# A third row pair of gate and up in seven products, and the sum T of each block's outer pairs in a tile of its own

## The chip, the cores and the metric

One NeuronCore of a Trainium2 chip runs the whole program. The metric is the time of one execution on the device in microseconds (us), the median of several runs.

## The reference

A trunk of two residual layers on 256 tokens of width 2048, in float32. Each layer has a token mixer (a gated linear recurrence in layer 0, gated linear attention in layer 1) with a cross-attention beside it, an output projection, and a SwiGLU feed-forward part. The change touches the feed-forward part alone:

```python
D_MODEL = 2048
SEQ = 256
DEPTH = 2
D_FF = ((8 * D_MODEL // 3 + 255) // 256) * 256        # 5632

    for layer in range(DEPTH):
        ...
        hn = _rmsnorm(h, norm_ffn[layer])
        gate, up = jnp.split(hn @ w_gate_up[layer], 2, axis=-1)
        h = h + (jax.nn.silu(gate) * up) @ w_down[layer]
    return _rmsnorm(h, norm_final)
```

`w_gate_up` is 2048 x 11264 in each layer, `w_down` 5632 x 2048.

## The kernel before

**Matmuls.** Every float32 operand is split into a high part and the rest (`split`: ACT copies the high part in the rounded matmul type, DVE subtracts it). A product of two such operands takes three matmuls: high by high, high by rest, rest by high. Tokens are the stationary side, in 128 x 128 blocks; weights are the moving side, 512 columns wide.

**Gate and up.** `ffn` goes through 11 blocks of 512 columns of gate and the 512 columns of up that belong to them (`up_block`, `project_halves`). A block is a sum over 8 row pairs, each of 256 rows of the weights: two rows of 128 by two columns (gate c0, up c1), against two rows of tokens. Done plainly such a 2 x 2 by 2 x 2 product takes eight products of blocks. `KINDS` has a letter for each row pair of a block: S takes seven products (a Strassen scheme in Winograd's form, with sums and differences of the blocks), O and H take eight in two ways that end in the same seven sums. `KINDS[min(b, 4)]` is used, so blocks 4 to 10 share the last string. `PAIRS` says which combinations of the tokens are made ready for each row pair (`Forms`, 8 factors for S, 6 for O).

**A row pair in seven products.** `load_pair` fills a tile `raw` of four 512-wide columns: raw 0 and 3 are gate's two rows, raw 1 and 2 up's. The scheme needs T, the sum of up's two rows: SP loads the first row into raw 1, and POOL then issues a DMA that adds the second row to it in memory (`accum_op`, line 424), which has to wait until the first has landed. SP loads raw 0, 3 and 2 as well. `seven` then makes four splits, named a to d in the tiles: a and b of weights as loaded, then two subtractions in `raw` (the first reads T), then c (from raw 0 and T, with the sign turned) and d. So DVE has six operations for a pair in seven products and two for a plain O pair. Tiles are numbered by `n_w`, which counts every weight tile: `parts139c` is split c of weight tile 139, the pair whose loads go to `raw139`.

**Buffers.** There are three `raw` tiles in turn, six `parts` tiles (1024 wide, both parts), two `part` tiles (512 wide, split a alone). Eight PSUM banks hold the seven sums of a block (`f_p`) and the accumulators of the down projection (`fd`).

**Down projection.** After each block of gate and up stand two pieces of the down projection (`down`), each 2 x 4 weight rows onto a 512-wide part of h. ACT first copies h into the banks (`fd<-h`) and at the end back (`h<-fd`). The block's seven sums are added up on DVE (`sums`, `s` and `e`), gated (`gate`), and turned for later pieces. One of the subtractions of the down weights' splits goes to POOL (line 292, `free_port`), ordered behind the first of the sums.

**Order of work.** Each engine works through its queue in order. `mark` and `due` put the pieces at fixed keys, and `Engine.kept` has PE, DVE and ACT keep the written order in the blocks. DMAs issued from SP and from POOL stand in those engines' queues where a scheduler puts them, and a DMA whose wait is not over holds what is queued behind it.

The tile tag `scx` has one buffer. In the mixers it holds scores; in the feed-forward part it is not used.

Of the kernel before, what the change touches and what calls it, by code (L numbers as in the profile page):

```python
# [9 lines left out]
F32 = mybir.dt.float32  # L10
# [7 lines left out]
P = 128  # L18
T = 256
# [21 lines left out]
def trunk_kernel(ctx: ExitStack, tc: tile.TileContext, x, mem, norm_mix, norm_ffn, norm_mem,  # L41
# [234 lines left out]
    def split(src, name, by=2, turned=False):  # L276

        n, m = src.shape[1:]
# [81 lines left out]
    PAIRS = "SSOSSOSB"  # L360
# [51 lines left out]

    def load_pair(raw, w, p, c0, c1, n, kind, fed):

        if n_w[0] == 1:
            for k, j, c in ((0, 0, c0), (0, 1, c1), (1, 3, c0), (1, 2, c1)):
                nc.sync.dma_start(out=raw[:, j, 0:n], in_=w[(2 * p + k) * P:(2 * p + k + 1) * P, c:c + n])
                if k == 0 and c == c1:
                    load_mem(0, 256, 512)
            return  # L420
        if kind == "S" and fed:
            rows = [w[(2 * p + k) * P:(2 * p + k + 1) * P, c1:c1 + n] for k in range(2)]
            nc.sync.dma_start(out=raw[:, 1, 0:n], in_=rows[0])
            nc.gpsimd.dma_start(out=raw[:, 1, 0:n], in_=rows[1], accum_op=ALU.add)  # L424
        nc.sync.dma_start(out=raw[:, 0:4:3, 0:n], in_=w[2 * p * P:(2 * p + 2) * P, c0:c0 + n].rearrange("(k p) c -> p k c", p=P))
        if kind == "S" and fed:
            nc.sync.dma_start(out=raw[:, 2, 0:n], in_=rows[1])
        else:
            nc.sync.dma_start(out=raw[:, 1:3, 0:n], in_=w[2 * p * P:(2 * p + 2) * P, c1:c1 + n].rearrange("(k p) c -> p k c", p=P))

    def seven(i, raw, fed, between=None):
# [10 lines left out]
        tt(out=raw[:, 0, :], in0=raw[:, 1, :], in1=raw[:, 0, :], op=ALU.subtract)  # L442
        tt(out=raw[:, 2:4, :], in0=raw[:, 2:4, :], in1=raw[:, 0:1, :].broadcast_to([P, 2, n]), op=ALU.subtract)
        t6, t7 = split(raw[:, 0:2, :], f"{i}c", turned=True)
# [158 lines left out]
    def project_halves(forms, kinds, w, c0, c1, name, key, keep):  # L603
# [15 lines left out]
        for p, kind in enumerate(kinds):  # L619
            Engine.kept = keep <= p  # L620
            i, raw = new_raw()
            fed = True
# [551 lines left out]
    KINDS = ("SHOSHOSO", "HHOSSOSO", "SHOSSOSO", "SSOSSOHS", "SSOSSOSS")  # L1174
# [10 lines left out]
    def ffn(l, forms, r, after, tail=None):  # L1185
        sq = {}

        def up_block(b):
            ps = project_halves(forms, KINDS[min(b, 4)], w_gate_up[l], 512 * b, DFF + 512 * b, f"f{l}_{b}_",
                                100 * b, 0 if b else 3)  # L1190
# [55 lines left out]
        for b in range(DFF // 512):  # L1246
            up_block(b)
            todo += [(i, n) for i, part in enumerate(PARTS) if part[-1] == b - 1 for n in range(NQ)]
            for j in range(2):
                if todo:  # L1250
                    down(*todo.pop(0), 100 * b + 10 + 2 * j, 100 * b + WHEN[min(b, 3)]["back"][j])
# [150 lines left out]
```

## Time and profile before

| | |
|---|---|
| time, median of 3 runs (lowest to highest) | 2261.01 us (2260.9 to 2262.21) |
| the profiled execution: its time, its span | 2261.07 us, 2259.0 us |
| busy: PE, DVE, ACT, POOL | 99%, 87%, 63%, 9% |
| DMA | 473.60 MB, mean 210 GB/s |
| chain that ended last: PE, DVE, DMA, issue | 94%, 2%, 1%, 1% |
| blocks 4 to 9 of layer 0, start to start | 62.1 us each |
| one such block: DVE busy, ACT busy, POOL busy | 55.6, 40.1, 7.7 us |

Times in the timelines are in us from the start of the span. A row of a timeline has its start, its length, the engine, the line, the operation, what it writes and reads, the shapes, and how many were merged; in brackets, if there is one, the idle time of the engine before it and what ended that. Nearly all operations of PE, DVE and ACT have line 151, which is a helper that issues them, so rows are told apart by their tiles. The start of one row to the start of the next on the same engine is the step, a little less than the length, since the ends overlap.

### The profile page before, as it was taken

To read this page: it belongs to the slowest core of one execution; us is meant where nothing else is said; L and a number is where in the kernel's file an instruction comes from. 1 tells how busy PE (TensorE), PEld (TensorE's weight loads), DVE (VectorE), ACT (ScalarE), POOL (GpSimd) and SP (SyncE) were. 2 spreads that over 40 slices of the span, in tenths; PEclk is the share of its full clock that TensorE was granted. 3 is DMA by queue.
4 is the path that set the end of the run, shared out by engine and by line. 5 is a ranking of instruction groups with operands and counts; after the bars stand their busy time and mean duration, and the time that the engine had idled before them with its cause. 6 is when DMAs were issued, how large, how long until landed. Compare 5 with 4: busy or idle time off the path is not lost.

```text
span 2259.0 us, 30203 instructions
## 1 busy us (share of the span) xinstructions
PE 2245.2 (99%) x10710; PEld 1903.1 (84%) x10710; DVE 1974.4 (87%) x2459; ACT 1425.3 (63%) x1938; POOL 202.3 (9%) x205
## 2 busy tenths in 40 slices
PE   9999999999999999999999999999999999999998
PEld 7888888888888888888889999988888888888887
DVE  6889899898898989988986887889889898888987
ACT  7656656565666666665665665566566666666664
POOL 1000100000111111111100000000011111111110
PEclk9999999999999999999999999999999999999999
DMA  8656655665676777777765455566677777777774
GB/s 295 215 169 212 203 182 171 196 196 182 210 241 213 244 234 216 228 233 227 232 216 171 137 165 182 166 205 200 201 230 226 227 232 222 230 228 220 240 235 155
DMA packets 255691, 473.60 MB, mean 210 GB/s; under 512 B 17807, under 2 KB 47283, under 8 KB 255283
## 3 DMA queue, kind: packets, MB, share of 16 engines
q1 hardware_dynamic: 233507, 429.65, 56.8%
q0 software_dynamic: 20736, 37.76, 10.5%
q10 hardware_dynamic: 1296, 4.26, 0.5%
q8 instruction: 84, 1.38, 0.2%
q14 instruction: 68, 0.56, 0.1%
HBM read 468.45 MB, written 3.15 MB: 209 GB/s over the span
## 4 chain that ended last, share of the span: by engine, by line
PE 94%; DVE 2%; issue 1%; DMA 1%; ACT 0%; SPq 0%; POOLq 0%; DVEq 0%; POOL 0%; ACTq 0%
PE f_p L151 37%; PE fd L151 17%; PE wo L151 4%; PE m1p L151 2%; PE hv2p L151 2%; PE hv1p L151 2%; PE hv0p L151 2%; PE hf0p L151 2%; PE wo0p L151 2%; PE wo1p L151 2%; PE hf2p L151 2%; PE hf1p L151 2%; PE m0p L151 2%; PE gk0p L151 1%; PE gk1p L151 1%; PE gg11p L151 1%
## 5 line engine op out<-in xcount | busy, mean ns | idle before, releaser
L151 DVE TENSOR_TENSOR raw<-raw 128x512 f32<-128x512 f32 (+3 forms) x330 | 303.7, 921 | 49.8 <-DMA raw<-in_w_gate_up_dram 30.9
L151 ACT CAST parts<-raw 128x1024 fp32r<-128x1024 f32 (+1 forms) x216 | 212.2, 1017 | 48.5 <-PE gx L151 6.3
L151 DVE TENSOR_TENSOR parts<-raw,parts 128x1024 fp32r<-128x1024 f32 (+1 forms) x196 | 223.9, 1176 | 20.2 <-ACT parts L151 20.0
L424 POOL DMA_DIRECT2D raw<-in_w_gate_up_dram x114 | 98.8, 867 | 960.9 <-DMA raw<-in_w_gate_up_dram 348.6
L151 ACT COPY h<-fd 128x512 f32<-128x512 f32 x80 | 46.2, 588 | 84.6 <-PE fd L151 81.7
L292 POOL TENSOR_TENSOR parts<-raw,parts 128x1024 fp32r<-128x1024 f32 x20 | 48.7, 2433 | 232.6 <-ACT parts L151 219.0
L151 ACT ACTIVATE s<-s,rf_r 128x512 f32<-128x512 f32 x44 | 31.8, 723 | 44.0 <-DVE s L151 43.9
L151 DVE TENSOR_TENSOR e<-f_p,e 128x512 f32<-128x512 f32 x66 | 45.1, 684 | 2.3
L151 ACT COPY fd<-h 128x512 f32<-128x512 f32 x82 | 45.3, 585 | 0.0
L151 PE MATMUL fd<-parts,s_0h 128*128 128x512 f32 x128 | 39.8, 392 | 0.0
L151 PE MATMUL fd<-parts,s_8h 128*128 128x512 f32 x128 | 39.8, 392 | 0.0
L151 PE MATMUL fd<-parts,s_6h 128*128 128x512 f32 x128 | 39.8, 392 | 0.0
L151 PE MATMUL fd<-parts,s_4h 128*128 128x512 f32 x128 | 39.8, 392 | 0.0
L151 PE MATMUL fd<-parts,s_2h 128*128 128x512 f32 x128 | 39.8, 392 | 0.0
L151 PE MATMUL fd<-parts,s_5h 128*128 128x512 f32 x128 | 39.4, 389 | 0.0
L151 PE MATMUL fd<-parts,s_1h 128*128 128x512 f32 x128 | 39.4, 389 | 0.0
L151 PE MATMUL fd<-parts,s_7h 128*128 128x512 f32 x128 | 39.4, 389 | 0.0
L151 PE MATMUL fd<-parts,s_3h 128*128 128x512 f32 x128 | 39.4, 389 | 0.0
L151 DVE TENSOR_TENSOR s<-f_p,e 128x512 f32<-128x512 f32 x44 | 30.3, 688 | 10.0 <-PE f_p L151 8.1
L424 POOL DMA_DIRECT2D raw<-in_hgrn_w_in_dram x17 | 14.8, 874 | 210.8 <-DMA raw<-in_hgrn_w_in_dram 125.6
L151 DVE SCALAR_TENSOR_TENSOR s<-e,rf_r,s 128x512 f32<-128x512 f32 x44 | 31.0, 745 | 0.2
L151 PEld LDWEIGHTS fd<-parts,s_1h 128*128 128x128 f32 x128 | 24.0, 188 | 5.0
(5728 smaller groups left out, 7298.9 us busy)
## 6 DMA issues: line engine op xcount, KB each, us to landing
raw<-in_w_gate_up_dram SPq DMA_DIRECT2D x238, 512.0 KB, 4.8
raw<-in_w_down_dram SPq DMA_DIRECT2D x80, 1024.0 KB, 5.9
raw<-in_w_gate_up_dram SPq DMA_DIRECT2D x228, 256.0 KB, 4.0
raw<-in_hgrn_w_in_dram SPq DMA_DIRECT2D x79, 512.0 KB, 4.8
raw<-in_gla_w_in_dram SPq DMA_DIRECT2D x96, 384.0 KB, 3.9
raw<-in_w_gate_up_dram POOLq DMA_DIRECT2D x114, 256.0 KB, 5.3
raw<-in_w_out_dram SPq DMA_DIRECT2D x16, 1024.0 KB, 5.4
raw<-in_w_mem_kv_dram SPq DMA_DIRECT2D x27, 512.0 KB, 5.5
```

Of the source, the lines that this page charges most:

```text
L151: ins = func(*args, **kwargs)
L292: low = (nc.gpsimd if free_port else ve).tensor_tensor(out=both[:, 1, k:j, 0:m], in0=src[:, k:j, :], in1=both[:, 0, k:j, 0:m].bitcast(F32) ...
L424: nc.gpsimd.dma_start(out=raw[:, 1, 0:n], in_=rows[1], accum_op=ALU.add)
```

## The change

Three things change together.

1. Row pair 2 (the third) is made ready for seven products (`PAIRS`) and runs in seven in blocks 4 to 10 of each layer. In blocks 0 to 3 it runs as H, in eight products, since the factors for O are no longer there.
2. For pair 0 of a block, and for pair 7 where that is in seven products, T is no longer made in `raw` 1. `load_apart` issues from POOL a load of up's first row into a tile of its own (tag `scx`, named T) and the adding load of the second row. For pair 0 of the next block this is written after the present block's products, for pair 7 at pair 4 of the same block.
3. `split` takes such a pair's c in two operations of 512 on each engine in place of one of 1024, T's half first.

```diff
     def split(src, name, by=2, turned=False):
 
+        if isinstance(src, list):
+            both = wts.tile([P, 2, 2, 512], F32R, tag="parts", name=f"parts{name}", bufs=6)
+            for k in (1, 0):
+                hi = both[:, 0, k:k + 1, :]
+                ac.activation(out=hi, in_=src[k], func=AF.Copy, scale=-1.0)
+                ve.scalar_tensor_tensor(out=both[:, 1, k:k + 1, :], in0=src[k], scalar=-1.0, in1=hi.bitcast(F32),
+                                        op0=ALU.mult, op1=ALU.subtract)
+            return [(both[:, 0, k, :], both[:, 1, k, :]) for k in range(2)]
...
-    PAIRS = "SSOSSOSB"
+    PAIRS = "SSSSSOSB"
...
+    def column(w, p, c1, n):
+        return [w[(2 * p + k) * P:(2 * p + k + 1) * P, c1:c1 + n] for k in range(2)]
+
+    def load_apart(w, p, c1):
+
+        both = work.tile([P, 1, 512], F32, tag="scx", name=f"T{n_w[0]}_{p}")
+        rows = column(w, p, c1, 512)
+        nc.gpsimd.dma_start(out=both[:, 0, :], in_=rows[0])
+        nc.gpsimd.dma_start(out=both[:, 0, :], in_=rows[1], accum_op=ALU.add)
+        return both
...
         if kind == "S" and fed:
-            rows = [w[(2 * p + k) * P:(2 * p + k + 1) * P, c1:c1 + n] for k in range(2)]
-            nc.sync.dma_start(out=raw[:, 1, 0:n], in_=rows[0])
-            nc.gpsimd.dma_start(out=raw[:, 1, 0:n], in_=rows[1], accum_op=ALU.add)
+            rows = column(w, p, c1, n)
+            if fed is True:
+                nc.sync.dma_start(out=raw[:, 1, 0:n], in_=rows[0])
+                nc.gpsimd.dma_start(out=raw[:, 1, 0:n], in_=rows[1], accum_op=ALU.add)
...
-        tt(out=raw[:, 0, :], in0=raw[:, 1, :], in1=raw[:, 0, :], op=ALU.subtract)
+        apart = fed if fed and fed is not True else None
+        tt(out=raw[:, 0, :], in0=apart[:, 0, :] if apart else raw[:, 1, :], in1=raw[:, 0, :], op=ALU.subtract)
...
-        t6, t7 = split(raw[:, 0:2, :], f"{i}c", turned=True)
+        t6, t7 = split([raw[:, 0:1, :], apart] if apart else raw[:, 0:2, :], f"{i}c", turned=True)
...
-            fed = True
+            if p == 4 and kinds[7] == "S":
+                apart[7] = load_apart(w, 7, c1)
+            fed = apart.get(p, True)
...
-    KINDS = ("SHOSHOSO", "HHOSSOSO", "SHOSSOSO", "SSOSSOHS", "SSOSSOSS")
+    KINDS = ("SHHSHOSO", "HHHSSOSO", "SHHSSOSO", "SSHSSOHS", "SSSSSOSS")
...
+        ready = {}
+
+        def first(b):
+            if KINDS[min(b, 4)][0] != "S":
+                return {}
+            return ready.pop(b, None) or {0: load_apart(w_gate_up[l], 0, DFF + 512 * b)}
...
             up_block(b)
+            if b + 1 < DFF // 512:
+                ready[b + 1] = first(b + 1)
```

How that moves instructions is shown for block 5 of layer 0: weight tiles 136 to 143 are its pairs 0 to 7, 144 to 147 the four of the two pieces of the down projection after it, 148 and on the next block's pairs.

On DVE, pair 2 (tile 138) before, from the end of pair 1 to the start of pair 3:

```order
L151 TENSOR_TENSOR parts137d_6581<-raw137_6559,parts137d_6581 128x1024
L151 TENSOR_TENSOR parts138a_6608<-raw138_6605,parts138a_6608 128x1024
L151 TENSOR_TENSOR parts138b_6611<-raw138_6605,parts138b_6611 128x1024
L151 TENSOR_TENSOR parts139a_6643<-raw139_6638,parts139a_6643 128x512
L151 TENSOR_TENSOR parts139b_6646<-raw139_6638,parts139b_6646 128x1024
```

and now:

```order
L151 TENSOR_TENSOR parts137d_6627<-raw137_6605,parts137d_6627 128x1024
L151 TENSOR_TENSOR parts138a_6656<-raw138_6651,parts138a_6656 128x512
L151 TENSOR_TENSOR parts138b_6659<-raw138_6651,parts138b_6659 128x1024
L151 TENSOR_TENSOR raw138_6651<-raw138_6651 128x512
L151 TENSOR_TENSOR raw138_6651<-raw138_6651 128x1024
L151 SCALAR_TENSOR_TENSOR parts138c_6664<-raw138_6651,parts138c_6664 128x1024
L151 TENSOR_TENSOR parts138d_6667<-raw138_6651,parts138d_6667 128x1024
L151 TENSOR_TENSOR parts139a_6696<-raw139_6691,parts139a_6696 128x512
L151 TENSOR_TENSOR parts139b_6699<-raw139_6691,parts139b_6699 128x1024
```

Two splits of 1024 have become the six operations of a pair in seven products; PE has 171 matmuls for the block where it had 174.

On POOL's queue, the same block before, from pair 3's adding load to the next block's first (line 424 issues adding loads, line 292 is the subtraction for the down projection):

```order
L424 DMA raw139_6638<-in_w_gate_up_dram 128x512
L424 DMA raw140_6678<-in_w_gate_up_dram 128x512
L424 DMA raw142_6751<-in_w_gate_up_dram 128x512
L424 DMA raw143_6791<-in_w_gate_up_dram 128x512
L292 TENSOR_TENSOR parts145_0_6879<-raw145_6877,parts145_0_6879 128x1024
L424 DMA raw148_6995<-in_w_gate_up_dram 128x512
```

and now (lines 428 and 429 are the plain and the adding load of `load_apart`, T141_7 for pair 7 of this block, T144_0 for pair 0 of the next; line 444 was 424, line 300 was 292):

```order
L444 DMA raw138_6651<-in_w_gate_up_dram 128x512
L428 DMA T141_7_6732<-in_w_gate_up_dram 128x512
L429 DMA T141_7_6732<-in_w_gate_up_dram 128x512
L444 DMA raw139_6691<-in_w_gate_up_dram 128x512
L444 DMA raw140_6731<-in_w_gate_up_dram 128x512
L444 DMA raw142_6807<-in_w_gate_up_dram 128x512
L428 DMA T144_0_6887<-in_w_gate_up_dram 128x512
L429 DMA T144_0_6887<-in_w_gate_up_dram 128x512
L300 TENSOR_TENSOR parts145_0_6938<-raw145_6936,parts145_0_6938 128x1024
L444 DMA raw149_7101<-in_w_gate_up_dram 128x512
```

The loads for T141_7 stand ahead of pair 3's adding load, and those for T144_0 between pair 6's and POOL's subtraction. The second of each two waits in the queue until the first has landed, and the first until the tile's reader before is done, since both T's take the one buffer of `scx`.

More of the change, by code (lines that the diff above doesn't have):

```diff
@@ L601, in project_two, with project_halves @@
             add(to, b, to)
-    def project_halves(forms, kinds, w, c0, c1, name, key, keep):
+    def project_halves(forms, kinds, w, c0, c1, name, key, keep, apart):
         left = {b: sum(TIMES[kind][b - 1] for kind in kinds) for b in range(1, 8)}
@@ L1186, in ffn @@
         sq = {}
+        ready = {}
[3 more added lines that the diff above has]
+            return ready.pop(b, None) or {0: load_apart(w_gate_up[l], 0, DFF + 512 * b)}
         def up_block(b):
             ps = project_halves(forms, KINDS[min(b, 4)], w_gate_up[l], 512 * b, DFF + 512 * b, f"f{l}_{b}_",
-                                100 * b, 0 if b else 3)
+                                100 * b, 0 if b else 3, first(b))
             when = WHEN[min(b, 3)]
```

## The prediction

> **What bounds the kernel now.** I read the page first, for the shares of the engines; then the chain that ended last, for the engine that carries the end; then the busy time stretch by stretch; and last the timelines of one steady block, engine by engine, for how far each runs ahead.
>
> ```profile
> span 2259.0 us, 30203 instructions
> PE 2245.2 (99%) x10710; PEld 1903.1 (84%) x10710; DVE 1974.4 (87%) x2459; ACT 1425.3 (63%) x1938; POOL 202.3 (9%) x205
> ...
> 790.59 39.44 PE f_p L151 x174
> 830.03 16.32 PE fd L151 x72
> 847.23 5.46 PE fd L151 x24
> 852.69 39.44 PE f_p L151 x174
> ...
> 516.40:601.38 84.98, 84.98 (x384) 70.30 (x383) 74.30 (x89) 51.96 (x66) 8.20 (x8) 1.00 0.71 220
> ...
> 790.43:852.52 62.09, 62.09 (x279) 51.50 (x278) 55.62 (x59) 40.10 (x50) 7.73 (x8) 1.00 0.75 229
> ```
>
> PE's 99% alone proves little, since ends of matmuls are modelled. The chain does: in a steady block of gate and up, 174 matmuls `f_p` stand in it without a gap, 39.44/174 = 0.2267 us each, and the next block's come 62.10 us later. The last row, the stretch of one such block (its figures are PE, PEld, DVE, ACT and POOL, then PE's clock, DMA's share and GB/s), has PE full at clock 1.00, DVE busy 55.62 of 62.09, ACT 40.10. So a matmul less is 0.2267 us less, until another engine is late; the one to watch is DVE, with 6.47 us to spare in each block.
>
> Blocks 4 to 10 of both layers run like this one: 14 blocks. I count from B = 790.43, where PE starts the block's first product. DVE's rows from there (raw tiles 136 to 143 are pairs 0 to 7, 144 to 147 the down projection's four, 148 the next block's first; a, b, c, d are the splits of a pair):
>
> ```profile
> 792.26 1.23 DVE L151 SCALAR_TENSOR_TENSOR parts137c<-raw,parts137c 128x1024 fp32r<-128x1024 f32 x1 [0.97 <-ACT parts137c L151]
> 794.54 1.22 DVE L151 TENSOR_TENSOR parts138a<-raw,parts138a 128x1024 fp32r<-128x1024 f32 x1
> ...
> 796.81 0.68 DVE L151 TENSOR_TENSOR parts139a<-raw,parts139a 128x512 fp32r<-128x512 f32 x1
> 797.41 1.22 DVE L151 TENSOR_TENSOR parts139b<-raw,parts139b 128x1024 fp32r<-128x1024 f32 x1
> 798.55 1.94 DVE L151 TENSOR_TENSOR raw<-raw 128x512 f32<-128x512 f32 x2
> 800.50 1.22 DVE L151 SCALAR_TENSOR_TENSOR parts139c<-raw,parts139c 128x1024 fp32r<-128x1024 f32 x1
> 801.69 1.23 DVE L151 TENSOR_TENSOR parts139d<-raw,parts139d 128x1024 fp32r<-128x1024 f32 x1
> 802.83 0.69 DVE L151 TENSOR_TENSOR parts140a<-raw,parts140a 128x512 fp32r<-128x512 f32 x1
> ...
> 805.36 1.95 DVE L151 TENSOR_TENSOR raw<-raw 128x512 f32<-128x512 f32 x2 [0.71 <-DMA raw<-in_w_gate_up_dram]
> ...
> 809.65 1.22 DVE L151 TENSOR_TENSOR parts141a<-raw,parts141a 128x1024 fp32r<-128x1024 f32 x1
> ...
> 820.67 1.95 DVE L151 TENSOR_TENSOR raw<-raw 128x512 f32<-128x512 f32 x2 [0.90 <-DMA raw<-in_w_gate_up_dram]
> 822.63 1.22 DVE L151 SCALAR_TENSOR_TENSOR parts143c<-raw,parts143c 128x1024 fp32r<-128x1024 f32 x1
> ...
> 827.23 0.68 DVE L151 TENSOR_TENSOR s<-f_p,e 128x512 f32<-128x512 f32 x1
> ...
> 832.01 1.22 DVE L151 TENSOR_TENSOR parts<-raw,parts 128x1024 fp32r<-128x1024 f32 x1
> 834.47 4.62 DVE L151 TENSOR_TENSOR parts<-raw,parts 128x1024 fp32r<-128x1024 f32 x4
> 842.14 0.69 DVE L151 TENSOR_TENSOR parts148a<-raw,parts148a 128x512 fp32r<-128x512 f32 x1 [3.05 <-ACT parts148a L151]
> ```
>
> A pair in seven products costs DVE 802.83 - 796.81 = 6.02 us when nothing is late; a plain pair (138) 796.81 - 794.54 = 2.27. Waits are the rest: 0.97, 0.71, 0.90 and 3.05. PE's rows for the same tiles, and the two engines around the down projection:
>
> ```profile
> 790.43 0.61 PE L151 MATMUL f_p<-parts136a,hf_0h 128*128 128x512 f32 x2
> 812.19 0.61 PE L151 MATMUL f_p<-parts140c,hf_4h 128*128 128x512 f32 x2
> 826.47 0.61 PE L151 MATMUL f_p<-parts143c,hf_7h 128*128 128x512 f32 x2
> 829.87 0.61 PE L151 MATMUL fd<-parts,s_3h 128*128 128x512 f32 x2
> 835.31 0.61 PE L151 MATMUL fd<-parts,s_4h 128*128 128x512 f32 x2
> ...
> 790.01 1.27 ACT L151 COPY h<-fd 128x512 f32<-128x512 f32 x2 [2.31 <-PE fd L151]
> 826.47 1.11 ACT L151 COPY fd<-h 128x512 f32<-128x512 f32 x2
> 827.51 2.00 ACT L151 CAST parts<-raw 128x1024 fp32r<-128x1024 f32 x2
> ...
> 812.03 15.68 SPq L303 DMA_DIRECT2D raw<-in_w_down_dram  x4
> ...
> 813.13 0.86 POOL L424 DMA_DIRECT2D raw<-in_w_gate_up_dram  x1 [5.76 <-DVE parts142a L151]
> 828.65 2.40 POOL L292 TENSOR_TENSOR parts<-raw,parts 128x1024 fp32r<-128x1024 f32 x1 [14.66 <-ACT parts L151]
> ```
>
> DVE is done with 140c at 805.36 + 1.95 + 1.22 = 808.53 and PE takes it at 812.19: a lead of 3.66 us. At the last pair 143c ends at 822.63 + 1.22 = 823.85 and is taken at 826.47: 2.62. These leads are the whole reserve inside a block.
>
> **What the change removes.** Pair 2 goes from eight products to seven: 3 matmuls, 3 x 0.2267 = 0.68 us a block, 14 x 0.68 = 9.52 us, all of it on PE and on the path. In blocks 0 to 3 pair 2 turns from one form in eight products into another in eight: no matmul changes; two DVE operations come, a subtraction and a split of 512, about 0.6 each as row 139a's step to 139b, 1.2 us for each of 8 blocks. Pair 2's factors grow from six to eight once a layer, under 1 us of DVE. I cost both at nothing: a pair of 24 matmuls lasts 5.44 us on PE against 2.27 + 1.2 on DVE, and the first block with its neighbours (the stretch from 516.40) has DVE idle for 10.7 us of 84.98 and PE for none. Were that cover gone, 8 x 1.2 + 2 would be 11.6 us.
>
> **What it adds to DVE.** In each of the 14 blocks pair 2 costs 6.02 in place of 2.27: 3.75 us. The split c of pairs 0 and 7 becomes two operations of 512; no row has that form on its own, so the bounds are half of c's step, 0.60, and a whole one, 1.19; the step of the 512-wide a (0.60) is nearest: two of them 1.20 against 1.19, nothing. DVE then works 59.4 of a block's 61.41 (62.09 - 0.68). It fits in sum; whether it fits in order is the question. ACT gains three splits of 512, 1.5 by the row at 827.51, on 40.10 and is not the bound. SP loses a row load in pairs 0 and 7 and gains one in pair 2; POOL issues two plain loads and one accumulate more (pair 2's; those of pairs 0 and 7 go to the new tile), 0.86 each as row 813.13; 0.25 MB more on DMA engines that are busy for 0.75 of the block.
>
> **The order, pair by pair.** DVE cannot run further ahead at the block's start: 137c waits for ACT, whose row at 790.01 waits for PE's last `fd`. That anchors pair 2 at B + 4.11 (794.54), before and after. From there, without waits: pair 3 at 10.13, pair 4 at 16.15, its c (3.69 into a pair) done at 16.15 + 3.69 + 1.22 = 21.06. PE wants it after 4 x 21 + 9 = 93 matmuls, 21.08. Pair 5 starts at 22.17, 6 at 24.44, 7 at 30.46. There T in its own tile is split first, raw's half second: done at 30.46 + 3.69 + 0.60 + 0.69 = 35.44, where PE wants that half after 156 matmuls at 35.37. How soon PE follows DVE shows where PE did wait:
>
> ```profile
> 8.25 0.69 DVE L151 TENSOR_TENSOR parts0a<-raw,parts0a 128x512 fp32r<-128x512 f32 x1 [1.04 <-ACT parts0a L151]
> 8.99 0.50 PE L151 MATMUL m0p<-parts0a,mem0h 128*128 128x512 f32 x1 [0.23 <-DVE parts0a L151]
> ```
>
> 8.94 to 8.99, 0.05. So PE is held 0.03 at pair 4 and 0.12 in all by pair 7; with steps of 0.67 for the halves it would be 0.25. I take 0.13 a block, of bounds 0 and 0.25.
>
> **The waits on DMA.** 0.71 and 0.90 go. 143's T comes ahead in its own tile. 140's wait came from an accumulate that took long because a plain pair frees its buffer only 2.27 us after and the next 1 MB is asked for at once; now seven-product pairs stand 6.02 apart. What is late next is pair 6, whose buffer is freed at 16.25 by pair 3. Its T was ready to issue on POOL 813.13 - 809.65 = 3.5 us after a free, so at 19.8. The accumulates land:
>
> ```profile
> raw<-in_w_gate_up_dram POOLq DMA_DIRECT2D x1, 256.0 KB, 4.4
> ...
> raw<-in_w_gate_up_dram POOLq DMA_DIRECT2D x1, 256.0 KB, 5.0
> ...
> raw<-in_w_gate_up_dram POOLq DMA_DIRECT2D x1, 256.0 KB, 7.5
> ```
>
> (issued at 789.84, 836.59 and 813.13). The 7.5 had 1 MB of down weights asked for just ahead of it, SP's row at 812.03; pair 6 will have nothing new until 22.3. With 4.4 to 5.0 it is there by 24.8, wanted at 30.46 - 6.02 + 1.74 = 26.18: no wait. The new accumulate for pair 2 starts from a buffer that the down projection frees some 10.9 before B and is wanted at 5.85: 16.7 us, for 3.5 and at most 7.5.
>
> **POOL's queue.** T for the next block's pair 0 waits for its tile to be read in pair 7 (34.15 + 0.69 = 34.84), is loaded, and the accumulate on it must wait on POOL until the load has landed; behind these two stands POOL's subtraction for the first down projection, now released by ACT at 828.5. Load issued at 34.9; for a plain load from POOL no row stands, so its landing is bounded by the accumulates' 4.4 and 7.5, and I take 5.0, the one that ran with a load issued some 3 us ahead; accumulate 0.86, subtraction 2.40: done at 43.2. PE wants the tile 5.44 (835.31 - 829.87) after the down projection's start, which moves to 38.76 + 0.13 = 38.89: 44.33. Cover 1.1 us. The other T, for pair 7, is asked for when pair 0's split c has read the tile (842.14 + 3.69 + 0.60, 6.1 before the next B) and holds pair 3's accumulate behind it to about B; with 7.5 that lands by 8.4 and is wanted at 11.87.
>
> **Down projection.** DVE gets to the sums at 36.5 + 2.3 = 38.8 in place of 36.80, leaves them 4.8 later, and needs 7.1 more (832.01 to 839.09), 50.7. The next block's first split stood at 842.14, B + 51.71, held by ACT; it moves to 51.2. The 3.05 wait shrinks to 0.5, the anchor holds. ACT's two copies into the down projection's banks ended at 827.58, 4.96 after pair 7's subtractions (820.67 + 1.95); now 34.15 + 4.96 = 39.11, and PE needs the second three matmuls in, at 39.57.
>
> By the Trainium skill, page "SBUF — State Buffer", section "Who interferes with whom", a DVE instruction with two SBUF inputs and a GpSimd instruction that reads SBUF exclude each other, one waiting for the whole of the other. By that rule the subtraction is safe beside the sums, which read PSUM, and 2.40 in the row that lies beside them agrees; it would be shut out if it started past 43.6, where DVE's next split begins. By the rows the sum holds no such term; by the rule each block in which that happens costs up to a split more.
>
> **Sum.** 14 x (0.68 - 0.13) = 7.7. The profiled execution took 2261.07, as the median of the runs (2261.01): 2253.4 us.
>
> **Rivals.** No wait at all: 2261.0 - 9.5 = 2251.5; for it speaks that 0.13 is made of hundredths. Part of the gain lost: a hold between 0.36 and 1.0 a block, from small waits on ACT or DMA in the dense 30 us of DVE; 2256.5 to 2265.5, about 2260. Slower, first way: pair 6's accumulate takes 7.5; T at 27.35 in place of 26.18, a hold of 1.3, 14 x (1.3 - 0.68) = 8.7, so 2269.7; it decides from a wait of 0.55, a landing of 6.9; against it, nothing large is asked for just before. Slower, second way: the load of T takes 7.5 on POOL's path, the subtraction ends at 45.66, PE is held 1.33 + 0.13, 14 x (1.46 - 0.68) = 10.9, so 2271.9; it decides at a landing of 6.7. Third, the subtraction starts late and DVE's splits of 1.22 shut it out: a hold of 2.68, 28 us, so 2289; it needs a start past 43.6, a landing over 7.8, and no row has one. It is the skill's rule above that would make it so.
>
> **Chances.** Forecast with a hold up to 0.36: 0.62. No hold: 0.06. Part lost: 0.17. Pair 6's accumulate: 0.07. POOL's queue: 0.06. The subtraction shut out: 0.02. About 0.2% (4.5 us) is what a measurement here can tell from no change: faster 0.68, same 0.17, slower 0.15. The range runs from 2250.5, just under no hold, to 2264.5 and leaves out the slower cases and the edge of the third. Within the forecast alone it is 2251.5 to 2256.5.
>
> **What would show it.** 10668 matmuls; steady blocks 61.5 us apart; DVE busy 59.4 in each, its wait ahead of the next block's first split about 0.5; gaps of PE of about 0.1 at c of pairs 4 and 7 and none at the second quad of the down projection; no DVE wait on DMA inside a block. A wait of PE for POOL's tile, or of DVE for pair 6's T, of over 0.6 a block would make the forecast wrong.

## The result, and the profile after

The changed kernel took 2256.8 us (median of 11 runs, 2254.9 to 2258.65) against 2261.22 for the kernel before on the same chip (11 runs, 2260.45 to 2262.58): a ratio of 0.9979, 95% interval 0.997 to 0.9987. It is faster by 4.4 us, where 7.7 had been forecast; the time lies 3.4 us above the predicted 2253.4 and inside the range, but just above 2256.5, where the forecast's own band ended and its rival "part of the gain lost" began. The profiled execution took 2256.8 as well, its span is 2254.7. One run of a later set of the changed kernel took 5072.13 us, and that set's ratio leaves it out.

The page of the changed kernel, the chain of work around two steady blocks, and two rows of busy time by stretch (one steady block, then blocks 0 and 1 of layer 0; columns as before), with blocks 0 and 1 of the kernel before as the last row:

```profile
span 2254.7 us, 30364 instructions
PE 2238.9 (99%) x10668; PEld 1893.9 (84%) x10668; DVE 2037.5 (90%) x2571; ACT 1453.5 (64%) x2010; POOL 233.5 (10%) x255
...
792.66 38.81 PE f_p L151 x171
...
854.13 38.81 PE f_p L151 x171
...
792.50:853.97 61.47, 61.47 (x277) 50.94 (x276) 59.24 (x65) 41.67 (x54) 9.61 (x10) 1.00 0.79 230
517.73:615.68 97.95, 97.47 (x439) 79.83 (x438) 87.69 (x106) 61.14 (x81) 7.21 (x7) 1.00 0.62 196
516.27:612.99 96.72, 96.72 (x439) 80.10 (x438) 84.83 (x101) 60.20 (x78) 8.33 (x8) 1.00 0.66 206
```

10668 matmuls are 42 fewer, 14 x 3. A steady block is 854.13 - 792.66 = 61.47 us long in place of 62.10, and PE is still full in it. But blocks 0 and 1, which lost no matmul, became 1.23 us longer, and there PE now has idle time: 97.95 - 97.47 = 0.48, not counting rows that the wait made longer.

In DVE's rows of the steady block (pairs 0 to 7 are tiles 136 to 143, B = 792.50) the reader finds pair 2 in seven products, c of pair 4 and of pair 7, and the end of the down projection's splits. Below them stand PE's rows for the same splits, and POOL's for T of the next block and its subtraction:

```profile
796.61 0.68 DVE L151 TENSOR_TENSOR parts138a<-raw,parts138a 128x512 fp32r<-128x512 f32 x1
...
812.34 1.23 DVE L151 SCALAR_TENSOR_TENSOR parts140c<-raw,parts140c 128x1024 fp32r<-128x1024 f32 x1
...
826.57 0.68 DVE L151 SCALAR_TENSOR_TENSOR parts143c<-T,parts143c 128x512 fp32r<-128x512 f32 x1
827.18 0.68 DVE L151 SCALAR_TENSOR_TENSOR parts143c<-raw,parts143c 128x512 fp32r<-128x512 f32 x1
...
841.29 2.36 DVE L151 TENSOR_TENSOR parts<-raw,parts 128x1024 fp32r<-128x1024 f32 x2 [0.43 <-ACT parts L151]
843.73 0.69 DVE L151 TENSOR_TENSOR parts148a<-raw,parts148a 128x512 fp32r<-128x512 f32 x1
```
```profile
813.58 0.63 PE L151 MATMUL f_p<-parts140c,hf_4h 128*128 128x512 f32 x2
...
814.28 0.62 PE L151 MATMUL f_p<-parts140c,hf_4h 128*128 128x512 f32 x2
...
827.91 0.61 PE L151 MATMUL f_p<-parts143c,hf_7h 128*128 128x512 f32 x2
...
828.59 0.61 PE L151 MATMUL f_p<-parts143c,hf_7h 128*128 128x512 f32 x2
```
```profile
827.56 0.57 POOL L428 DMA_DIRECT2D T<-in_w_gate_up_dram  x1 [14.71 <-DVE parts143c L151]
830.73 0.86 POOL L429 DMA_DIRECT2D T<-in_w_gate_up_dram  x1 [2.61 <-DMA T<-in_w_gate_up_dram]
832.28 2.41 POOL L300 TENSOR_TENSOR parts<-raw,parts 128x1024 fp32r<-128x1024 f32 x1 [0.69 <-ACT parts L151]
```

140c ends at B + 21.07 and PE takes it at B + 21.08; 143c's second half ends at B + 35.36 and is taken at B + 35.41. The forecast had 21.06 against 21.08 and 35.44 against 35.37. These are PE's first products of each split, which need only the high part that ACT makes; the second product, one step of 0.23 later, is the first that needs DVE's rest. The hold is 61.47 - 61.41 = 0.06 us a block. PE's rows show it at pair 4 alone: there three products step 814.28 - 813.58 = 0.70, at pair 7 three step 828.59 - 827.91 = 0.68.

Where the 4.3 us of the two spans came from, by the start of each block's first product `f_p`:

| stretch | before | after | difference |
|---|---|---|---|
| start to block 0 of layer 0 | 516.27 | 517.73 | +1.46 |
| blocks 0 and 1, each layer | 96.72 | 97.95 | +1.23, twice |
| blocks 2 and 3, each layer | 115.35 | 115.35 | 0 |
| blocks 4 to 9, layer 0 and layer 1 | 372.56, 372.56 | 368.80, 368.77 | -3.76, -3.79 |
| block 10 of layer 0 to block 0 of layer 1 | 461.16 | 460.66 | -0.50 |
| block 10 of layer 1 to the end | 112.32 | 112.14 | -0.18 |

The steady blocks brought what the forecast said and a little more. In this profile 2.5 us went in blocks 0 and 1, 1.5 ahead of layer 0's block 0, and 1.0 in the last block. The experiments take these one by one.

### The profile page after: what moved, and what is told of

It reads as the page before. It is cut to its first block, busy times and chain, and to the rows that moved or that the text cites. A ratio compares the mean times of both kernels' runs of the same rounds, so it can differ in the third digit from the quotient of the medians.

```text
span 2254.7 us, 30364 instructions
## 1 busy us (share of the span) xinstructions
PE 2238.9 (99%) x10668; PEld 1893.9 (84%) x10668; DVE 2037.5 (90%) x2571; ACT 1453.5 (64%) x2010; POOL 233.5 (10%) x255
## 4 chain that ended last, share of the span: by engine, by line
PE 83%; DVE 9%; issue 3%; DMA 2%; ACT 1%; POOL 0%; SPq 0%; DVEq 0%; POOLq 0%; ACTq 0%
PE f_p L151 33%; PE fd L151 17%; PE wo L151 4%; PE m1p L151 2%; PE hf0p L151 2%; PE wo1p L151 2%; PE hf1p L151 2%; PE hv0p L151 2%; PE wo0p L151 2%; PE m0p L151 2%; PE hv2p L151 1%; PE gk0p L151 1%; PE gk1p L151 1%; PE gg11p L151 1%; PE gg10p L151 1%
## 5 line engine op out<-in xcount | busy, mean ns | idle before, releaser
L151 DVE TENSOR_TENSOR raw<-raw 128x1024 f32<-128x1024 f32 (+3 forms) x330 | 311.4, 944 | 12.5 <-DMA raw<-in_hgrn_w_in_dram 2.6
L444 POOL DMA_DIRECT2D raw<-in_w_gate_up_dram x92 | 80.4, 874 | 577.9 <-DMA raw<-in_w_gate_up_dram 263.7
L428 POOL DMA_DIRECT2D T<-in_w_gate_up_dram x36 | 22.6, 627 | 436.3 <-DVE hf_4g L151 84.3
L429 POOL DMA_DIRECT2D T<-in_w_gate_up_dram x36 | 31.0, 861 | 122.7 <-DMA T<-in_w_gate_up_dram 105.1
```

The lines of the kernel that those rows point to most:

```text
L151: ins = func(*args, **kwargs)
L428: nc.gpsimd.dma_start(out=both[:, 0, :], in_=rows[0])
L429: nc.gpsimd.dma_start(out=both[:, 0, :], in_=rows[1], accum_op=ALU.add)
```

## Experiments

### The two halves of the change by themselves

The first kernel keeps pair 2 in seven products and takes the T tiles away, the second keeps the tiles and takes the seven products away:

```diff
 seven_only:
-            if KINDS[min(b, 4)][0] != "S":
+            if True:
                 return {}
-            if p == 4 and kinds[7] == "S":
+            if False:
                 apart[7] = load_apart(w, 7, c1)
 t_only:
-    PAIRS = "SSSSSOSB"
+    PAIRS = "SSOSSOSB"
-    KINDS = ("SHHSHOSO", "HHHSSOSO", "SHHSSOSO", "SSHSSOHS", "SSSSSOSS")
+    KINDS = ("SHOSHOSO", "HHOSSOSO", "SHOSSOSO", "SSOSSOHS", "SSOSSOSS")
```

Without the tiles:

> The changed kernel without its T tiles: pair 2 in seven products as changed, but T of pairs 0 and 7 made in raw 1 again, c of those pairs split in one operation. Theory (T's own tile carries pair 7): T of pair 7 can be loaded only when pair 4's split d has freed the buffer, about 22.1 us into the block; its accumulate goes out some 3.5 later and lands after 4.4 to 7.5, at 30.0 to 33.1, while DVE wants it at 32.2. DVE has 0.05 us to spare there, so a steady block loses between 0 and 0.9 us, about 0.5: 62.0 us apart in place of 61.47, and about 2264 us. Rival (the tiles are worth nothing, the accumulate is in time anyway): 61.47 us apart, 2256 to 2257 us.

Measured: 2271.87 us (2269.89 to 2277.83), 1.0047 of the kernel before, 95% 1.0034 to 1.0059. So the seven products alone, with all 42 matmuls gone, make the kernel slower. In the profile one block still takes 61.43, others up to 63.0. Such a block, with DVE's wait in it and PE's:

```profile
918.21:981.19 62.98, 62.02 (x276) 50.86 (x275) 59.25 (x63) 41.61 (x52) 8.49 (x8) 1.00 0.78 229
```
```profile
951.96 1.95 DVE L151 TENSOR_TENSOR raw<-raw 128x512 f32<-128x512 f32 x2 [1.45 <-DMA raw<-in_w_gate_up_dram]
```
```profile
955.19 0.50 PE L151 MATMUL f_p<-parts167c,hf_7h 128*128 128x512 f32 x1 [0.76 <-DVE parts167c L151]
```

The place is the expected one, pair 7, but DVE's wait was 1.45, more than the 0.9 allowed, so the size was underestimated (2264 expected).

At the end of block 1 of layer 0 this run also shows something that the changed kernel does not: one of DVE's splits of the down weights meets POOL's subtraction. DVE's row, then POOL's:

```profile
605.63 2.11 DVE L151 TENSOR_TENSOR parts<-raw,parts 128x1024 fp32r<-128x1024 f32 x1
```
```profile
603.92 2.73 POOL L300 TENSOR_TENSOR parts<-raw,parts 128x1024 fp32r<-128x1024 f32 x1
```

The split took 2.11 where the same form takes 1.22, and ended 607.74 - 606.65 = 1.09 after POOL's subtraction: it waited for that to end. At the same place in layer 1 the split took 1.75, and ended 1.09 after the subtraction there too.

The tiles without the seven products:

> The kernel before with T of pairs 0 and 7 in tiles of their own and c in halves; PAIRS and KINDS as before, so pair 2 stays plain everywhere. Theory (the 1.23 us that blocks 0 and 1 of each layer lost come from H at pair 2, which asks more of DVE than O): blocks 0 and 1 together take 96.7 us as before in both layers, steady blocks 62.1, so 2261 to 2262 us. Rival (the loss comes from the T tiles, their loads and their places in POOL's queue): blocks 0 and 1 take 97.95 us here too, about 2263.7 us.

Measured: 2262.0 us (11 runs), 0.9999 of the kernel before, 95% 0.999 to 1.0008. Blocks 0 and 1 of layer 0 and a steady block:

```profile
517.99:614.71 96.72, 96.72 (x440) 80.10 (x439) 84.87 (x102) 60.35 (x79) 7.70 (x8) 1.00 0.65 203
792.15:854.24 62.09, 62.09 (x280) 51.50 (x278) 55.77 (x61) 40.38 (x52) 8.68 (x9) 1.00 0.79 228
```

Both as before, so the tiles did not lengthen blocks 0 and 1. They bring nothing where PE is full anyway. The gain belongs to neither half alone: the seven products use up DVE's reserve, and the tiles keep the transfers from asking for any.

### What blocks 0 and 1 lost

In block 1 three pairs are H. DVE's rows of pair 2 (tile 94) and of pair 4's c (tile 96) in the changed kernel, and PE's for the latter; then c of pair 4 in the kernel before:

```profile
571.87 0.69 DVE L151 TENSOR_TENSOR raw<-raw 128x512 f32<-128x512 f32 x1
573.33 0.69 DVE L151 TENSOR_TENSOR parts94c<-raw,parts94c 128x512 fp32r<-128x512 f32 x1 [0.77 <-ACT parts94c L151]
...
584.35 1.22 DVE L151 SCALAR_TENSOR_TENSOR parts96c<-raw,parts96c 128x1024 fp32r<-128x1024 f32 x1
...
585.63 0.50 PE L151 MATMUL f_p<-parts96c,hf_4h 128*128 128x512 f32 x1 [0.39 <-DVE parts96c L151]
```
```profile
579.45 1.22 DVE L151 SCALAR_TENSOR_TENSOR parts96c<-raw,parts96c 128x1024 fp32r<-128x1024 f32 x1
...
582.86 0.62 PE L151 MATMUL f_p<-parts96c,hf_4h 128*128 128x512 f32 x2
```

Before, 96c was done at 580.67 and PE wanted its rest with the second of its two matmuls, 0.23 after 582.86: a lead of 2.42 us. Now DVE is 584.35 - 579.45 = 4.90 later there, of which 1.46 is the later start of layer 0's blocks: 3.44 in place of a cover of 2.42. An H at pair 2 costs DVE more than the two operations of 0.6, since the split of the difference waits for ACT's copy of it, 0.77. The remedy takes the difference ahead of split b, so that ACT copies it while DVE does b:

```diff
                 b00, b01 = split(raw[:, 0:2, :], f"{i}a")
                 mark(key + p)
+                if kind == "H":
+                    ve.tensor_tensor(out=raw[:, 0, :], in0=raw[:, 3, :], in1=raw[:, 2, :], op=ALU.subtract)
                 b11, b10 = split(raw[:, 2:4, :], f"{i}b")
 ...
-                    ve.tensor_tensor(out=raw[:, 3, :], in0=raw[:, 3, :], in1=raw[:, 2, :], op=ALU.subtract)
-                    e1, = split(raw[:, 3:4, :], f"{i}c")
+                    e1, = split(raw[:, 0:1, :], f"{i}c")
```

> The changed kernel with one step of form H moved: the difference of the second row's two columns is taken ahead of split b, into raw 0 (already split), in place of behind it, into raw 3. DVE then need not wait for ACT between the subtraction and split c. Theory (DVE falls behind in block 1, where three pairs are H, and each H costs it 0.6 + 0.7 wait + 0.6): the three waits of about 0.7 go, more than the 1.03 us that PE lost at pairs 3 and 4 of block 1; blocks 0 and 1 take 96.7 to 96.9 us in both layers, about 2254.5 us. Rival (the loss of blocks 0 and 1 is not H's wait but a transfer or the work of DVE in sum): 97.5 to 97.95 us remain, 2256 to 2257 us.

Measured: 2255.32 us (6 runs), 0.9968 of the kernel before, 95% 0.9956 to 0.998. DVE's rows of pair 2 now follow one another, and 96c is ready before PE asks; blocks 0 and 1 take 96.87 in both layers:

```profile
570.62 0.69 DVE L151 TENSOR_TENSOR raw<-raw 128x512 f32<-128x512 f32 x1
571.24 1.22 DVE L151 TENSOR_TENSOR parts94b<-raw,parts94b 128x1024 fp32r<-128x1024 f32 x1
572.37 0.69 DVE L151 TENSOR_TENSOR parts94c<-raw,parts94c 128x512 fp32r<-128x512 f32 x1
...
584.39 1.22 DVE L151 SCALAR_TENSOR_TENSOR parts96c<-raw,parts96c 128x1024 fp32r<-128x1024 f32 x1
```
```profile
586.22 0.62 PE L151 MATMUL f_p<-parts96c,hf_4h 128*128 128x512 f32 x2
...
519.49:616.36 96.87, 96.87 (x440) 80.00 (x438) 86.73 (x105) 61.16 (x80) 8.07 (x7) 1.00 0.63 197
```

1.08 of the 1.23 us came back in each layer. The edit takes the wait out of every H, also out of the two that block 1 had before, so it shows that DVE's time in H was at fault; that the loss came with the H at pair 2, `t_only` shows. The theory holds and the rival falls: with H mended, the four profiles that have it and both tiles take 96.86 to 96.90 in both layers. Without it the loss is not always 1.23: two more profiles with the old H and both tiles, below, show 97.31 or 97.32 three times and 97.91 once. In the dearer case (layer 0 of the changed kernel's first profile) DVE had waited another 0.52 us for ACT at block 1's first split, and with no lead left that wait went on to PE. So H costs 0.6 us in each layer by itself, and 1.2 where something else is late.

### How much room DVE has left

> The changed kernel with pair 5 made ready for seven products too: KINDS[4] is all S, and H stands at pair 5 of blocks 0 to 3. Theory (DVE has 2 us a block left and no more): PE's work in a steady block falls by another 0.68 to 60.8 us, but DVE's rises by 3.75 to 63.1, so blocks stand at least 63.1 us apart, and each of 14 loses 1.7 us: 24 us slower than the changed kernel, about 2281 us, and a few us more from four H in block 1. Rival (PE still bounds, DVE's sum has more room than it looks): blocks 60.8 apart, about 2247 us.

Its edit:

```diff
-    PAIRS = "SSSSSOSB"
+    PAIRS = "SSSSSSSB"
-    KINDS = ("SHHSHOSO", "HHHSSOSO", "SHHSSOSO", "SSHSSOHS", "SSSSSOSS")
+    KINDS = ("SHHSHHSO", "HHHSSHSO", "SHHSSHSO", "SSHSSHHS", "SSSSSSSS")
```

Measured: 2314.26 us (4 runs), 1.023, 95% 1.0216 to 1.0243. A steady block, and PE's waits at c of pairs 5 and 7:

```profile
864.52:929.62 65.10, 62.23 (x274) 50.15 (x272) 62.87 (x69) 43.57 (x56) 11.13 (x12) 1.00 0.79 227
```
```profile
891.66 0.50 PE L151 MATMUL f_p<-parts153c,hf_5h 128*128 128x512 f32 x1 [0.76 <-DVE parts153c L151]
...
903.65 0.50 PE L151 MATMUL f_p<-parts155c,hf_7h 128*128 128x512 f32 x1 [1.30 <-DVE parts155c L151]
```

DVE bounds, as the theory said, but a block is 65.1 long, over the floor of 63.1: DVE's busy 62.87 is what was expected, and on top of it come waits of DVE for ACT (0.97 ahead of 149c, 0.37 and 0.26 around the next block's first splits) that a sum of busy time leaves out. With one more pair in seven products the kernel lost 52 us against the kernel before.

### POOL's queue ahead of block 0, and the start

T of a layer's first block has a free tile long before, so its plain load was issued from POOL ahead of the small operation `ro_r` for which the output projection's operands wait. In the changed kernel (DVE, then POOL), and with that load ordered behind both `ro_r`:

```profile
440.27 1.13 DVE L151 SCALAR_TENSOR_TENSOR gates<-po,ro_r,gates 128x128 f32<-128x128 f32 x4 [1.89 <-POOL ro_r L189]
...
438.61 0.57 POOL L428 DMA_DIRECT2D T<-in_w_gate_up_dram  x1 [56.38 <-DVE ro_v L151]
439.19 1.05 POOL L189 TENSOR_TENSOR ro_r<-ro_v,mhalf 128x4 f32<-128x4 f32 x1
```
```profile
439.31 1.13 DVE L151 SCALAR_TENSOR_TENSOR gates<-po,ro_r,gates 128x128 f32<-128x128 f32 x4 [1.22 <-POOL ro_r L191]
...
441.63 0.63 POOL L430 DMA_DIRECT2D T<-in_w_gate_up_dram  x1
```

> The changed kernel with one edit: the plain load of a layer's first T is ordered on POOL behind the two small operations ro_r. Theory (DVE waited 1.9 us twice for ro_r in place of 1.2, because that load of 0.57 stood ahead of the first one): these two waits are about 1.2 again, and PE's first products of the output projection come without the 0.4 to 0.6 us that they lost against the kernel before; about 2256.3 us. Rival (the load has nothing to do with it): the waits stay at 1.9.

The edit gives `load_apart` the name of that operation:

```diff
-        nc.gpsimd.dma_start(out=both[:, 0, :], in_=rows[0])
+        plain = nc.gpsimd.dma_start(out=both[:, 0, :], in_=rows[0])
+        if behind:
+            tc.add_manual_dep(plain.ins, behind, ...)
```

One execution, 2255.62 us, span 2253.5. The first wait is 1.22 again (the second 1.19, both as in the kernel before). From PE's first product of the output projection to its first one with `y_2l`, which waits for these operands, the kernel before takes 24.44 us. The five profiles of kernels that issue that load early show 24.80 (the changed kernel), 24.83, 25.02, 25.45 and 25.53; the eight others 24.41 to 24.44. From the same start to block 0's first product it is 94.49 us in the kernel before, 95.00 in the changed kernel, 95.00 to 95.73 in those five profiles and 94.47 to 94.51 in the eight others. So the load costs 0.5 to 1.2 us, 0.5 of it in the changed kernel's first profile, which leaves 0.95 of the 1.46 us. Part of that cost is at the second `ro_r`: in the changed kernel an adding load of the output projection's weights stands ahead of it on POOL (441.40), in `first_behind` behind it (442.25), so the edit moved more than one load. Six of the eight profiles have pair 2's two added factors and two have not, so these cost nothing that shows.

> The kernel before, unchanged, for a second profile. Theory (0.9 of the 1.46 us that the changed kernel was late at its first block arose in the recurrence's mixer, where both kernels issue the same work in the same order: it is variation from run to run): its first block starts elsewhere than at 516.27, by some tenths to 2 us, with the steps at the products slh that follow the exponentials. Rival (the change does it): 516.2 to 516.4 again.

Measured: 2260.22 us, span 2258.2; its first block starts at 516.41, so by this stretch the expectation missed: it hardly moved. But the stretch from block 10 of layer 0 to layer 1, with the other mixer in it, took 460.17 in place of 461.16 with nothing changed. And over all 13 profiles, whose instructions up to that point are the same, the products `slh` of layer 0's mixer begin at 187.20 to 189.86 (187.63 in the first profile of before, 188.11 in that of the changed kernel). What differs ahead of them is when weights land. ACT in the kernel before and in `h_ahead`, at the same instruction:

```profile
175.20 1.05 ACT L151 CAST parts30a<-raw 128x1024 fp32r<-128x1024 f32 x1 [1.33 <-DMA raw<-in_hgrn_w_in_dram]
...
176.68 1.05 ACT L151 CAST parts30a<-raw 128x1024 fp32r<-128x1024 f32 x1 [2.33 <-DMA raw<-in_hgrn_w_in_dram]
```

So one profile's mixers vary by 1 to 2 us through their transfers. Whether the changed kernel's are later on average stays open: the two profiles of before start block 0 at 516.3 and 516.4, those of kernels without the early load at 516.5 to 518.6.

### POOL's queue in the last block, and a mended kernel

In the last block of layer 1 (tiles 400 to 407, B = 2142.56) the plain load of T for pair 7, issued at 2139.34, landed 8.2 us later, its adding load had to wait for it on POOL, and pair 3's adding load stood behind that, though pair 3's own first row was there. POOL's rows (the bracket of the first names another load that landed at nearly the same time), then DVE's and PE's at pairs 3 and 4:

```profile
2147.85 0.86 POOL L429 DMA_DIRECT2D T<-in_w_gate_up_dram  x1 [7.62 <-DMA raw<-in_w_gate_up_dram]
2148.46 1.14 POOL L444 DMA_DIRECT2D raw<-in_w_gate_up_dram  x1
```
```profile
2155.50 1.95 DVE L151 TENSOR_TENSOR raw<-raw 128x512 f32<-128x512 f32 x2 [0.99 <-DMA raw<-in_w_gate_up_dram]
```
```profile
2164.76 0.50 PE L151 MATMUL f_p<-parts404c,hf_4h 128*128 128x512 f32 x1 [0.74 <-DVE parts404c L151]
```

The block's 171 products took 39.83 us where a steady block's take 38.81. The profile of `h_ahead` lost as much in the same block (39.85), but at another load: there pair 3's adding load went out at B + 3.1, and pair 4's, with POOL idle ahead of it, at B + 11.1, 6.8 us after its first row had been asked for (2148.05).

The kernel `mended` joins three edits: H's difference ahead of split b, a layer's first T behind `ro_r`, and the plain load of T for pair 7 behind pair 3's adding load (`third` keeps the names of those):

```diff
+        if p == 7:
+            behind = third[-1]
+        if behind:
+            tc.add_manual_dep(plain.ins, behind, ...)
...
-                nc.gpsimd.dma_start(out=raw[:, 1, 0:n], in_=rows[1], accum_op=ALU.add)
+                third.append(nc.gpsimd.dma_start(out=raw[:, 1, 0:n], in_=rows[1], accum_op=ALU.add).ins.name)
```

> The changed kernel with three things mended: form H takes its difference ahead of split b; the plain load of T for pair 7 is ordered on POOL behind pair 3's accumulate; the plain load of a layer's first T is ordered behind the two small POOL operations (ro_r) that the output projection waits for. Theory: blocks 0 and 1 take 96.87 us as with the first of these alone (97.95 in the changed kernel), the last block loses the 0.74 us that PE waited at its pair 4, the front about 0.5; steady blocks stay at 61.43. Together 2 x 1.08 + 0.74 + 0.5 = 3.4 us less than the changed kernel: about 2253.5 us. Rival for the second step: T for pair 7, now issued later, lands late for pair 7 in some blocks, which then take 61.7 to 62.5; 2256 us.

Measured: 2253.57 us (6 runs, 2253.41 to 2255.88), 0.9966 of the kernel before, 95% 0.9954 to 0.9978: the lowest here, though its interval overlaps that of the changed kernel. Blocks 0 and 1 take 96.90 and 96.86, the front 516.53, and in the last block PE is not held. But two blocks of layer 1 lost 0.24 and 1.0. In the second (B = 1955.49) pair 4's adding load went out at B + 10.3, where the blocks on either side have it at B + 7.6, and it landed 8.6 us after. T's adding load for pair 7, now later on POOL, stood ahead of it until B + 9.3; but pair 4's own first row, asked for at 1959.71, landed 5.6 us later, at B + 9.8, so that without T it could hardly have gone earlier:

```profile
1964.82 0.85 POOL L438 DMA_DIRECT2D T<-in_w_gate_up_dram  x1 [5.16 <-DMA T<-in_w_gate_up_dram]
1965.83 0.85 POOL L453 DMA_DIRECT2D raw<-in_w_gate_up_dram  x1 [0.16 <-DVE parts366d L151]
...
1974.48 1.95 DVE L151 TENSOR_TENSOR raw<-raw 128x512 f32<-128x512 f32 x2 [1.02 <-DMA raw<-in_w_gate_up_dram]
```

The block took the 62.5 that the rival allowed, but at pair 4 and not at pair 7, and that T's later place caused it is not shown. Three kernels on one chip should tell whether that edit is worth having: the mended kernel, the same with its first two edits only, and the changed kernel.

> The mended kernel without its third edit: the plain load of T for pair 7 stands in POOL's queue ahead of pair 3's adding load again; H's difference ahead of split b and a layer's first T behind ro_r remain. Theory (the third edit only moves the hold: where the first row of pair 3 landed late, T's adding load held pair 4's instead, which was issued 10.3 us into the block in place of 7.6 and cost PE 1.02): the same time as the mended kernel within 1 us, about 2253.5 to 2254.5 us, with one or two blocks of 14 disturbed in either. Rival (the order matters, as the last block of the changed kernel suggested): 0.7 to 1 us or more slower than the mended kernel, from holds of pair 3's adding load in several blocks.

> The mended kernel again, beside the changed kernel and the one with two of the three edits. Theory: 2253.5 us, and 3 us under the changed kernel (two times 1.08 of blocks 0 and 1, 0.5 of the front, some tenths of late transfers). Rival (only the edit of H shows in the time): 1 to 2 us under the changed kernel.

> The changed kernel again, for a second profile and for times beside the mended ones. Theory: 2256.8 us, blocks 0 and 1 at 97.95 in both layers, steady blocks at 61.47, and another one or two blocks late than the last one of layer 1, since it is transfers that land late. Rival (the place in POOL's queue makes the last block of layer 1 late each time): block 10 of layer 1 loses 0.9 again.

| | median, us | ratio to before, 95% | blocks 0 and 1 | block 10 of layer 1 to the end |
|---|---|---|---|---|
| two edits | 2255.07 (7 runs) | 0.9972 (0.9961 to 0.9983) | 96.90, 96.88 | 112.16 |
| three edits | 2255.68 (8 runs) | 0.9974 (0.9964 to 0.9985) | 96.89, 96.86 | 110.94 |
| the changed kernel | 2257.68 (11 runs) | 0.9984 (0.9975 to 0.9993) | 97.31, 97.31 | 111.09 |

The order of T for pair 7 makes no difference in time that can be seen: the theory of `two_mended` held in that, and its rival fell. Both mended kernels came out above the 2253.5 to 2254.5 expected, and the 2253.57 of the set before, on another chip, did not come again. The 112.16 of the kernel with two edits is not the old hold: its 171 products of that block took 38.80 us, and PE lost 0.76 later, at a split of the down projection. The changed kernel's blocks 0 and 1 took 97.31 where 97.95 was expected. Its last block was not late this time (111.09, where 112.14 was measured first), so that loss is a transfer's, with POOL's queue as the place where it spreads, not a fixed cost. The mended kernels lie 2.0 and 2.6 us under the changed one, less than the 3 expected, and 2.0 is as much as the rival (only the edit of H shows) allows, so that the time alone does not show the other edits; all intervals of this set overlap, and what is firm are the two stretches of blocks 0 and 1 and the products `wo`, which repeat to hundredths.

### Whether pair 0 needs its tile

```diff
-            if KINDS[min(b, 4)][0] != "S":
+            if True:
                 return {}
```

(with H's difference ahead, as in `mended`; without pair 0's tile a layer's first T is that of pair 7 in block 4, so nothing stands ahead of `ro_r`).

> The changed kernel with the tile T for pair 7 alone (pair 0 makes T in raw 1 as before), with H's difference ahead of split b and the first T behind the small POOL operations. It tells what the tile for pair 0 is worth. Theory (only pair 7 needs it: without both tiles DVE waited 1.45 us for DMA at pair 7 and at no other pair of that block, and pair 0's c stands 7 us ahead of PE): steady blocks stay at 61.43 to 61.5, about 2253.5 us. Rival (pair 0's accumulate, now in POOL's queue behind the subtraction and ahead of pair 1's and 2's, makes DVE late at the block's start): over 61.7 a block, 2257 us and more.

Measured: 2268.44 us (9 runs), 1.0029, 95% 1.0019 to 1.0038. The theory fell. A block, DVE's wait at the subtraction of its pair 0 (tile 148), and PE's at c of its pair 4 (tile 152):

```profile
854.09:917.45 63.36, 62.18 (x277) 50.74 (x276) 59.99 (x65) 42.04 (x53) 9.04 (x9) 1.00 0.80 231
```
```profile
848.48 1.95 DVE L151 TENSOR_TENSOR raw<-raw 128x512 f32<-128x512 f32 x2 [2.59 <-DMA raw<-in_w_gate_up_dram]
```
```profile
877.19 0.50 PE L151 MATMUL f_p<-parts152c,hf_4h 128*128 128x512 f32 x1 [0.76 <-DVE parts152c L151]
```

Blocks over 61.7 us are what the rival had said, but not by its way: pair 0's adding load went out at 841.30, 3.8 us after its first row had been asked for (837.51) and with POOL idle for 6.45 us ahead of it, and took 7.1 us. Pair 0's c stands 7 us ahead of PE in the changed kernel and still matters: a wait of DVE there puts off everything that DVE does up to pair 4, where next to no reserve is left. Slack against PE at one split is no slack for DVE.

## Why the prediction was right, and where it was off

- **The gain on PE: right.** 42 matmuls fewer; a steady block shows 62.10 - 61.47 = 0.63 of the 0.68, fourteen times but for the two blocks 10, of which layer 0's lost 0.2 to a wait for ACT at pair 4 and layer 1's 1.0 to a late transfer.
- **The ledger of DVE inside a block: right.** From the anchor at B + 4.11 every split came where the sum of steps put it, 796.61 - 792.50 = 4.11 to begin with. DVE is busy 59.24 (59.4 forecast), its waits ahead of the next block come to 0.43 + 0.26 (0.5 forecast), pair 6 never waited for DMA. The hold was 0.06 in place of 0.13: the halves of 143c step 0.61 and 0.68 and end 0.08 earlier than I had put them. Worth 14 x 0.07 = 1.0 us to the good. The place of the hold was misjudged: most of it had been put at pair 7, and it came at pair 4 alone. I had set DVE's rest against PE's first product of a split, and the second is the one that needs it: it starts 813.81 - 813.57 = 0.24 after the end of 140c and 828.14 - 827.86 = 0.28 after that of 143c. Why 0.24 already lengthens PE's steps no run here shows.
- **Blocks 0 to 3 "at nothing": wrong, 2.5 us here (1.2 in the undisturbed profile).** This is the step that failed. It had the cover from PE's time for a pair (5.44 against 2.27 + 1.2) and from DVE's idle 10.7 us in a stretch of 84.98. Neither is the cover that counts, the lead at the tightest split, which the trace of before shows as 2.42 us at 96c; and an H costs 1.2 plus the 0.77 that DVE waits for ACT in its middle, with one in block 0 and one in block 1 before that split. Blocks 2 and 3, with the same H at pair 2, lost nothing, as the forecast had it. `t_only` and `h_ahead` show the cause by undoing each side of it.
- **POOL's queue in a steady block: right.** The adding load of T went out 830.73 - 827.56 = 3.2 us after the plain one (I took 5.0), the subtraction ended at B + 42.2 (43.2) against a need of 44.3, and PE was never held by it. It never started past 43.6, so the case in which the Trainium skill's rule on shared access (page "SBUF — State Buffer", section "Who interferes with whom") would have cost time did not come. The trace of `seven_only` agrees with the rule: there a split met POOL's subtraction and took 2.11 us in place of 1.22.
- **POOL's queue outside of it: left out, 0.5 us here, up to 1.2 elsewhere.** The prediction followed T for the next block and for pair 7, not T for a layer's first block, whose load stands ahead of `ro_r`. `first_behind` shows it.
- **T for pair 7 holding pair 3's adding load: bounded too tightly.** I had it held to about B and landed by 8.4, wanted at 11.87, with no landing over 7.5. In one block of 14 the plain load landed after 8.2 and pair 3's adding load was issued at B + 5.9: PE lost 1.0 us. It did not come again in the second profile.
- **Variation of transfers in the mixers: left out.** 1 to 2 us from profile to profile, which no step of mine could have given.

Added up, for the two first profiles: 7.7 + 1.0 (hold) - 2.5 (H) - 0.5 (`ro_r`) - 1.0 (last block) leaves 4.7; the spans differ by 4.3, and the 0.4 between lies in the front and the mixers (late transfers) and in layer 0's block 10, less a shorter end; it was not taken apart further. So the mechanism in the steady blocks was right, and the 3.4 us by which the time missed came from outside of them, from losses that none of the rivals named.

## What to carry to other kernels

When one engine feeds another in order, price an added operation, with the wait in its middle, against the lead at the tightest later hand-over, read from the two engines' rows, and not against idle time summed over a stretch. When such a lead is nearly gone, late transfers upstream of it turn into lost time, so look for what can be asked for earlier together with the saving. And give a DMA issued ahead of time its place in the queue by hand: a scheduler puts it as early as its buffer allows, which may be ahead of something small that others wait for.

## What the runs showed of the hardware that I had not expected

- A plain load of 256 KB issued from POOL takes 0.57 us of POOL where the adding one takes 0.86 (0.89 and 1.14 in the last block of layer 1, right behind another DMA). In the changed kernel such a load landed after 2.9 us in one place (issued at 827.56) and after 8.2 in another (2139.34).
- A DVE split with both inputs in SBUF that began while POOL's subtraction ran took 2.11 us in place of 1.22 (`seven_only`, 605.63).
- The same program took 461.16 and 460.17 us from block 10 of layer 0 to layer 1's first block, while its blocks with PE full repeated to 0.01 us.
